# The last layer's FFN as one group of 1024 tokens, with the gated activation kept in DRAM and the down projection summed in PSUM

## The chip, the cores and the metric

One core of a Trainium2 chip runs the whole program: TensorE (PE, with its weight loads as PEld), VectorE (DVE), ScalarE (ACT), GpSimd (POOL), SyncE (SP, which here only issues DMAs), on-chip SBUF, eight accumulation banks of PSUM (128 partitions x 512 fp32 columns each), and DRAM. The metric is the device time of one execution in microseconds (us), as the median of several runs. Beside the times stands one profiled execution with a record of every instruction.

## The reference

A backbone of two layers over 1024 latent tokens and 256 context tokens of width 1024, in fp32. Each layer mixes tokens (three head groups), projects the result (w_out), adds it gated to the stream, and then applies a gated MLP with 22 x 128 = 2816 features whose gate branch passes a centred convolution of width 3 along the tokens. Only latent tokens leave the last layer. In short form:

```python
h = rms_norm(x, g) * (1 + scale) + shift
gate, up = h @ w_gate, h @ w_up                  # (tokens, 2816) each
act = silu(dwconv3(gate, conv_w) + conv_b) * up  # the convolution runs along tokens
x = x + gate_mod * rms_norm(act @ w_down, g2)
```

## The kernel before

**Precision.** Every fp32 operand of a matmul is split into a high and a low part (`split`: a copy that rounds gives the high part, a subtraction the low one), and `mm3` (L246) issues three matmuls: high x high, high x low, low x high. So one product of blocks is three instructions.

**Gate and up.** `ffn` (from L1819) holds the normalised, modulated, transposed input in blocks: the first half of a group's tokens by two halves of the 1024 inputs ("11", "21"), the second half likewise ("22" and a difference "T3"), and from them `ffn_T` makes T1, T2 and T4 (tiles `T`, `ts`). Gate and up of one 128-feature block f are then got with seven products P1 to P7 (`PROD`) of combined weights and combined inputs instead of eight. Each product sums four 128-row blocks, so it takes 12 matmuls, and one f takes 84. The weights of f (`wraw`) are loaded, combined (L1857 to L1860) and split (`fwh`, `wl`, `fsh`, `fsl`) for each f of each group. VectorE combines the products out of PSUM into `fraw` and `fu` (`add`, L1877).

**Groups.** The last layer handles its 1024 tokens in two groups of 512 (tiles 2 to 5 and 6 to 9, 128 tokens each), each half of a group 256 columns and two more for the convolution's neighbours, so n = 258. The second group's input is prepared by `ffn_second` near the end of the first.

**Activation and down.** For each f: centre tap on GpSimd (L1933), the two other taps on VectorE (L1934, L1935), Silu on ScalarE, the multiply on VectorE (L1937), the split into `ahl`. After each pair of f, `down` multiplies the four token tiles with the two row blocks of w_down (`dr`, split into `dh` and `dl`): per tile and half of the output 6 matmuls of 512 columns into one bank, which VectorE then adds to an accumulator in SBUF (`yacc`, L1966 for the first pair, L1968 after that). Products use four banks ("m"), `down` the other four ("b"). `finish` normalises, scales, adds the residual (`res`) and stores.

**Around it.** Ahead of the FFN stands `outproj`: for each token tile 48 matmuls (tile `ow`, `yh`, `yl`), then `post` (L1574 to L1579: squares, an inverse root in small steps, gate, residual) and a store to DRAM (`scr_x`). `ffn_part` reloads the tiles, transposes them on PE (`hTp`) and splits them into the blocks. The instructions of each engine are put in order by a scheduler; buffers come from pools with a count for each name, so a load is issued once its buffer is free. All loads go through SP's queue, in order.

## Time and profile before

| what | value |
|---|---|
| median of 3 runs | 4708.21 us (4696.83 to 4727.73) |
| the profiled execution | 4714.89 us, span 4712.7 us |
| PE busy | 4242.9 us, 90% of the span |
| VectorE, GpSimd, ScalarE busy | 3227.4, 2328.2, 1849.2 us |
| last layer's FFN, first to last product | 3828.5 to 4691.8 us of the span |
| mean granted clock of PE | 0.887 |

The span is what the profiler saw between the first and the last instruction; the execution's own time lies 2.2 us above it. Busy shares are averages over stages that differ much, so the rows below are mostly cut to one stage. The granted clock is a share of full speed: 1.00 is the upper of two levels (2.4 GHz), 0.50 the lower (1.2 GHz), and a mean in between says that a stretch had both.

### The profile page before, as it was taken

Reading aid. Unit: us, or ns where it says so; the run is one execution under the profiler, and the core shown is the slowest. Engines: PE = TensorE matmul, PEld = TensorE weight load, DVE = VectorE, ACT = ScalarE, POOL = GpSimd, SP = SyncE. Lnnn points to the kernel's source line nnn. Section 1 sums busy time; section 2 is a strip of 40 time slices with the busy share of each in tenths; the row PEclk is TensorE's granted clock in tenths of the full one; section 3 lists DMA queues with packets and bytes.
Section 4 is the critical chain, followed back from the end, with each engine's and each line's share of the span. In section 5 each row is a group of like instructions: output and inputs, shape, how many; then the busy total and the mean of one; then the engine's idle time right before and its main releaser. Section 6 shows DMA issues by size and latency. Waiting matters only on the chain. (4 is left out here: it accounts for less than half of the span.)

```text
span 4712.7 us, 72125 instructions
## 1 busy us (share of the span) xinstructions
PE 4242.9 (90%) x26303; PEld 3318.7 (70%) x26303; DVE 3227.4 (68%) x6313; ACT 1849.2 (39%) x3692; POOL 2328.2 (49%) x2295
## 2 busy tenths in 40 slices
PE   8997988989999899979998997889899889997997
PEld 5885654755567799879986875567555678886886
DVE  4346586666655877887776257766777578888887
ACT  3334454543323333333333344555443233333332
POOL 3336225243443666566654243543444366657664
PEclk9996687885999999989998995879879989998998
DMA  6453223152123322232226453223411323223232
GB/s 206 131 141 99 59 75 97 49 142 60 31 78 116 103 81 81 86 112 86 81 85 165 124 134 83 65 54 77 121 56 29 112 101 90 81 85 107 87 90 85
DMA packets 501921, 441.26 MB, mean 94 GB/s; under 512 B 121652, under 2 KB 434108, under 8 KB 501566
## 3 DMA queue, kind: packets, MB, share of 16 engines
q1 hardware_dynamic: 448350, 381.45, 27.8%
q0 software_dynamic: 21056, 51.26, 4.1%
q10 hardware_dynamic: 32160, 3.94, 0.5%
q8 instruction: 208, 3.41, 0.3%
q14 instruction: 147, 1.20, 0.1%
HBM read 353.02 MB, written 83.51 MB: 93 GB/s over the span
## 5 line engine op out<-in xcount | busy, mean ns | idle before, releaser
L244 DVE TENSOR_TENSOR wl<-wraw,fwh 128x1024 fp32r<-128x1024 f32 x176 | 320.3, 1820 | 160.0 <-ACT fwh L238 159.5
L238 ACT ACTIVATE fwh<-wraw 128x1024 fp32r<-128x1024 f32 x264 | 272.4, 1054 | 297.1 <-DVE wraw L1860 156.7
L248 PE MATMUL m<-h,fwh 128*128 128x322 f32 (+1 forms) x1056 | 321.2, 304 | 15.4 <-ACT fu L1906 8.6
L248 PE MATMUL dn<-dh,ahl 128*128 128x512 f32 x792 | 315.4, 402 | 14.6 <-ACT ahl L238 10.0
L249 PE MATMUL dn<-dl,ahl 128*128 128x512 f32 x792 | 319.0, 403 | 8.8 <-POOL dl L244 8.8
L244 POOL TENSOR_TENSOR gp<-gx,gp 128x512 fp32r<-128x512 f32 x160 | 207.7, 1303 | 238.9 <-DVE gp L240 153.1
L250 PE MATMUL m<-h,wl 128*128 128x322 f32 (+1 forms) x1056 | 318.8, 302 | 4.3 <-DVE wl L244 4.3
L249 PE MATMUL m<-h,fwh 128*128 128x322 f32 (+1 forms) x1056 | 321.3, 304 | 0.0
L244 POOL TENSOR_TENSOR dl<-dr,dh 128x1024 fp32r<-128x1024 f32 x88 | 218.8, 2487 | 202.1 <-ACT dh L238 199.7
L1355 ACT ACTIVATE ds<-ds,dnm 128x512 f32<-128x512 f32 (+1 forms) x400 | 232.5, 581 | 185.2 <-DVE dnm L1377 105.6
L250 PE MATMUL dn<-dh,ahl 128*128 128x512 f32 x792 | 304.4, 399 | 0.0
L248 PE MATMUL m<-T,fwh 128*128 128x322 f32 (+1 forms) x704 | 220.4, 313 | 89.2 <-DVE fraw L1877 77.5
L244 POOL TENSOR_TENSOR wl<-wraw,fwh 128x1024 fp32r<-128x1024 f32 x88 | 229.3, 2606 | 122.8 <-ACT fwh L238 118.9
L1419 ACT ACTIVATE p<-ds 128x512 f32<-128x512 f32 (+1 forms) x336 | 186.8, 585 | 254.3 <-PE ds L1418 205.7
L1968 DVE TENSOR_TENSOR yacc<-dn,yacc 128x512 f32<-128x512 f32 x360 | 231.3, 681 | 28.0 <-PE dn L250 28.0
L244 POOL TENSOR_TENSOR ahl<-cv,ahl 128x642 fp32r<-128x642 f32 (+1 forms) x88 | 131.8, 1498 | 226.2 <-ACT ahl L238 203.4
L1936 ACT ACTIVATE cv<-cv 128x642 f32<-128x642 f32 (+1 forms) x88 | 60.6, 688 | 466.4 <-DVE cv L1935 466.4
L1377 DVE TENSOR_REDUCE dnm<-ds 128x1 f32<-128x512 f32 x256 | 173.7, 687 | 90.3 <-PE ds L1375 87.5
L244 DVE TENSOR_TENSOR wl<-wr,wh 128x512 fp32r<-128x512 f32 (+1 forms) x76 | 66.9, 882 | 242.2 <-ACT wh L238 151.0
L250 PE MATMUL m<-T,wl 128*128 128x322 f32 (+1 forms) x704 | 215.9, 307 | 8.5 <-DVE wl L244 8.5
L244 POOL TENSOR_TENSOR wl<-wr,wh 128x512 fp32r<-128x512 f32 (+1 forms) x76 | 100.3, 1319 | 244.6 <-ACT wh L238 175.2
L249 PE MATMUL m<-T,fwh 128*128 128x322 f32 (+1 forms) x704 | 217.3, 309 | 2.3 <-DVE T L244 2.3
(499 smaller groups left out, 13558.7 us busy)
## 6 DMA issues: line engine op xcount, KB each, us to landing
wraw<-in_ff_w_gate_dram SPq DMA_DIRECT2D x88, 512.0 KB
wraw<-in_ff_w_up_dram SPq DMA_DIRECT2D x88, 512.0 KB
dr<-in_ff_w_down_dram SPq DMA_DIRECT2D x88, 512.0 KB
aw<-in_ada_w_dram SPq DMA_DIRECT2D x160, 256.0 KB
wr<-in_w_in_dram SPq DMA_DIRECT2D x88, 256.0 KB
x<-scr_x SPq DMA_DIRECT2D x28, 512.0 KB
scr_df<-st SPq DMA_DIRECT2D x80, 128.0 KB
scr_gq<-st SPq DMA_DIRECT2D x18, 512.0 KB
```

Source lines behind the costliest of these rows:

```text
L238: nc.scalar.activation(hi, src, AF.Copy)
L244: e.tensor_tensor(out=lo, in0=src, in1=hi, op=ALU.subtract)
L248: mm(out, lh, rh, start=first, stop=False)
L249: mm(out, lh, rl, start=False, stop=False)
L250: mm(out, ll, rh, start=False, stop=last)
L1355: act.activation(s, s, AF.Exp, bias=nm[:, c, m, i:i + 1], accum_out=L[:, c, m, i:i + 1])
L1377: vv.tensor_reduce(out=nm[:, 1 + c, m, i:i + 1], in_=s, axis=AX.X, op=ALU.max, negate=True)
L1419: act.activation(p[:, m, :w], s[:, :w], AF.Exp)
L1936: act.activation(t[:, m], t[:, m], AF.Silu)
L1968: vv.tensor_tensor(out=ys[i][:, hs], in0=ps, in1=ys[i][:, hs], op=ALU.add)
```

## The change

Layer 0's code is kept; all that follows is for the last layer (l = 1).

- `FFN[1]` has one group of n = 512: blocks "11" and "21" hold tiles 2 to 5, "22" and "T3" tiles 6 to 9. Neighbour columns between groups, `edge` and `ffn_second` are not used there.
- The body of `steps` becomes `gate_up`, word for word but for three things: banks are taken from both sets in turn (`self.mb`), the split of the second weight pair has its low part on GpSimd, and q lies in `cv`.
- `ffn_last` runs gate and up for all 22 f, and `tail(f)` after each; it stores the gated activation, 128 features x 1024 tokens, to DRAM (`scr_act`). Then the down projection: two passes of four token tiles, in each over all 22 f with the sum held in the eight banks.
- The output projection's weights lie in `wo`; some of its pools and those of the attention before it get fewer buffers or other places (`ahl` 2 for 3, `y` in `fraw`); the last tile takes its two halves in the other order.

```diff
-        ((258, (((2, 3), ((0, 2, 0, 256),)), ((4, 5), ((1, 0, 0, 256),))),
-          ((0, 0), (0, 1), (1, 257)), (1, 256), 6),
-         (258, (((6, 7), ((0, 2, 0, 256),)), ((8, 9), ((1, 0, 0, 256),))),
-          ((0, 0), (1, 256), (1, 257)), (0, 1), None)),
+        ((512, (((2, 3), ((0, 0, 0, 256),)), ((4, 5), ((0, 256, 0, 256),)), ((6, 7), ((1, 0, 0, 256),)), ((8, 9), ((1, 256, 0, 256),))),
+          (), None, None),),
...
+    def gate_up(self, f, order, blk, res):
...
+            ps = P[p] = self.bk(next(self.mb))[:, :n]
...
+    def ffn_last(self, l, src, A, SH, blk, todo, rows):
...
+        def tail(f, raw, q):
+            w3 = [self.pt[:, 28 + NF * t + f:29 + NF * t + f] for t in range(3)]
+            t = ft([128, W], "cv", 4)
+            act.activation(t, raw, AF.Identity, scale=w3[1], bias=self.pt[:, 94 + f:95 + f])
+            vv.scalar_tensor_tensor(out=t[:, 1:W], in0=raw[:, 0:W - 1], scalar=w3[0], in1=t[:, 1:W], op0=ALU.mult, op1=ALU.add)
+            vv.scalar_tensor_tensor(out=t[:, 0:W - 1], in0=raw[:, 1:W], scalar=w3[2], in1=t[:, 0:W - 1], op0=ALU.mult, op1=ALU.add)
+            act.activation(t, t, AF.Silu)
+            gp.tensor_tensor(out=t, in0=q, in1=t, op=ALU.mult)
+            gp.dma_start(out=scr[f], in_=t)
+
+        res = [[], []]
+        st = [self.gate_up(f, self.FIRST, blk, res[f]) for f in range(2)]
+        next(st[0])
+        for t0, t1, p in todo:
+            rows(t0, t1)
+            K.together(p)
+        next(st[1])
+        yield
+        self.ffn_T(blk)
+        next(st[0])
+        for f in range(NF):
+            if f > 1:
+                res.append([])
+                st.append(self.gate_up(f, self.LAST if f == NF - 1 else self.ORDER, blk, res[f]))
+            K.together(st[f])
+            tail(f, *res[f])
+        yield
+
+        def operands(f, t0):
+            r, x = ft([128, D], "dr", 3), ft([128, 512], "ar", 3)
+            self.load(r, a["ff_w_down"][l, f * 128:f * 128 + 128, :])
+            self.load(x, scr[f][:, t0:t0 + 512])
+            g, d = ft([128, 2, 512], "ag", 3, F32R), ft([128, 2, D], "dd", 3, F32R)
+            self.split(d[:, 0], d[:, 1], r, "a", "v")
+            self.split(g[:, 0], g[:, 1], x, "a", "p")
+            return g, d
...
+        for t0 in (0, 4):
+            xs = []
+            for t in range(t0, t0 + 4):
+                xs.append(self.al("fB", [128, D], 8, n="res"))
+                self.load(xs[-1], self.xsrc(src, NCTX + t))
+            acc = [[self.bk(b) for b in ("m", "b")] for _ in range(4)]
...
+            for f in range(NF - 2):
+                g, d = operands(f, 128 * t0)
+                for i in range(4):
+                    products(i, f, g, d)
+                if late:
+                    end(*late.pop(0))
+            ops = [(f, *operands(f, 128 * t0)) for f in (NF - 2, NF - 1)]
+            for i in range(4):
+                for o in ops:
+                    products(i, *o)
+                y = acc[i]
+                if t0 == 0:
+                    s = self.al("hA0", [128, 2, 512], 8, n="ys")
+                    act.activation(s[:, 0], y[0], AF.Copy)
+                    vv.tensor_copy(s[:, 1], y[1])
+                    late.append((t0 + i, (s[:, 0], s[:, 1]), xs[i]))
+                else:
+                    end(t0 + i, y, xs[i])
```

`products` issues `mm3` for the two halves of the output of one tile; `end` is `finish` for one tile, in halves, out of PSUM or out of the copy `ys`.

What the scheduler makes of it is shown at three places. In each row stand line, operation, out<-in and shape.

**PE, start of the FFN.** Before, the last matmul of the output projection (`ow`, `yl`) and the first ones of P1 of f = 0 (`h` is the block "11"):

```order
L249 MATMUL b_36370<-ow_35297,yh_36258 128x512
L250 MATMUL b_36370<-ow_35297,yl_36259 128x512
L248 MATMUL m_36537<-h_35310,fwh_36514 128x258
L249 MATMUL m_36537<-h_35310,fwh_36514 128x258
L250 MATMUL m_36537<-h_35310,wl_36515 128x258
```

With the change the same place holds 36 products, P1 and P2 of f = 0 and P1 of f = 1, and then the transposes of tiles 8 and 9 (`x_36501`, `x_36504`); the rows begin with the last of the 36:

```order
L251 MATMUL m_36594<-h_35312,wl_36572 128x512
L1731 MATMUL hTp_36507<-ident,x_36501 128x128
L1731 MATMUL hTp_36512<-ident,x_36501 128x128
L1731 MATMUL hTp_36522<-ident,x_36501 128x128
L1731 MATMUL hTp_36527<-ident,x_36501 128x128
L1731 MATMUL hTp_36507<-ident,x_36504 128x128
```

Before, the transposes of a group's last tiles stood ahead of its products or, for the second group, among those of the first; now they stand between the first products of the only group.

**VectorE, one feature in the steady part.** Before, the weight split of `wl`, the combinations of 258 columns, the weight combinations (`wraw`) and the accumulators (`yacc`) follow each other:

```order
L1859 TENSOR_TENSOR wraw_43516<-ws_43524,wraw_43516 128x512
L1860 TENSOR_TENSOR wraw_43516<-wraw_43516 128x512
L1877 TENSOR_TENSOR fraw_43414<-fu_43330,m_43401 128x258
L244 TENSOR_TENSOR wl_43530<-wraw_43516,fwh_43529 128x1024
L1877 TENSOR_TENSOR fraw_43329<-fraw_43329,m_43416 128x258
L1877 TENSOR_TENSOR fraw_43414<-fu_43330,m_43416 128x258
L1968 TENSOR_TENSOR yacc_41134<-dn_43440,yacc_41134 128x512
L1968 TENSOR_TENSOR yacc_41134<-dn_43448,yacc_41134 128x512
L1968 TENSOR_TENSOR yacc_41151<-dn_43456,yacc_41151 128x512
L1968 TENSOR_TENSOR yacc_41151<-dn_43464,yacc_41151 128x512
L1934 SCALAR_TENSOR_TENSOR cv_43431<-fraw_43329,pt_23577,cv_43431 128x514
L1968 TENSOR_TENSOR yacc_41168<-dn_43472,yacc_41168 128x512
```

With the change, a whole feature:

```order
L1866 TENSOR_TENSOR fraw_37000<-fu_37001,m_37016 128x512
L245 TENSOR_TENSOR wl_37114<-wraw_37109,fwh_37113 128x1024
L1866 TENSOR_TENSOR fu_37001<-fu_37001,b_37030 128x512
L1848 TENSOR_TENSOR wraw_37109<-ws_37117,wraw_37109 128x512
L1866 TENSOR_TENSOR fraw_37000<-fu_37001,m_37044 128x512
L1849 TENSOR_TENSOR wraw_37109<-wraw_37109 128x512
L1866 TENSOR_TENSOR fu_37001<-fu_37001,b_37058 128x512
L1866 TENSOR_TENSOR cv_37085<-fu_37001,m_37072 128x512
L1866 TENSOR_TENSOR fraw_37000<-fraw_37000,b_37087 128x512
L1866 TENSOR_TENSOR cv_37085<-fu_37001,b_37087 128x512
L1934 SCALAR_TENSOR_TENSOR cv_37102<-fraw_37000,pt_23577,cv_37102 128x1023
L1935 SCALAR_TENSOR_TENSOR cv_37102<-fraw_37000,pt_23577,cv_37102 128x1023
```

The accumulators, one weight split and the multiply are gone from the queue; the combinations are 512 wide and the two taps 1023.

**SP, the end of gate and up.** Before, the loads of weights of gate and up (`wraw`) and of down (`dr`) and of the residuals (`res`) alternate to the end:

```order
L209 DMA dr_43852<-in_ff_w_down_dram 128x1024
L209 DMA wraw_44001<-in_ff_w_up_dram 128x8x128
L209 DMA wraw_44212<-in_ff_w_gate_dram 128x8x128
L209 DMA dr_43858<-in_ff_w_down_dram 128x1024
L209 DMA wraw_44213<-in_ff_w_up_dram 128x8x128
L209 DMA res_44348<-scr_x_102 128x1024
```

With the change, from the last weights of gate and up on:

```order
L210 DMA wraw_39387<-in_ff_w_gate_dram 128x8x128
L210 DMA wraw_39388<-in_ff_w_up_dram 128x8x128
L210 DMA gate_39527<-scr_mod_90 128x1024
L210 DMA res_39531<-scr_x_102 128x1024
L210 DMA res_39533<-scr_x_102 128x1024
L210 DMA res_39535<-scr_x_102 128x1024
L210 DMA res_39537<-scr_x_102 128x1024
L210 DMA res_40307<-scr_x_102 128x1024
L210 DMA res_40309<-scr_x_102 128x1024
L210 DMA res_40311<-scr_x_102 128x1024
L210 DMA dr_39547<-in_ff_w_down_dram 128x1024
L210 DMA ar_39548<-scr_act_36407 128x512
```

The down weights' loads all stand behind gate and seven residuals; the buffers of `dr`, `dd`, `ar` and `ag` come from a pool that opens when that of `T2`, `T14` and `cv` closes.

## Rows read from the trace of the kernel before

**Rows 1.** The page's first part: busy time, share of the span, instructions.

```profile
PE 4242.9 (90%) x26303; PEld 3318.7 (70%) x26303; DVE 3227.4 (68%) x6313; ACT 1849.2 (39%) x3692; POOL 2328.2 (49%) x2295
```

**Rows 2.** Timeline of PE: start us, us, instruction, out<-in, tile, shape.

```profile
3828.49 0.28 PE L248 MATMUL m<-h,fwh 128*128 128x258 f32 x1
...
4382.81 0.29 PE L248 MATMUL m<-T,fwh 128*128 128x258 f32 x1
...
4392.91 0.39 PE L248 MATMUL dn<-dh,ahl 128*128 128x512 f32 x1
4393.14 0.39 PE L249 MATMUL dn<-dl,ahl 128*128 128x512 f32 x1
...
4683.26 0.63 PE L248 MATMUL dn<-dh,ahl 128*128 128x512 f32 x1
4683.69 0.63 PE L249 MATMUL dn<-dl,ahl 128*128 128x512 f32 x1
```

**Rows 3.** Stretches of the last FFN: us, busy (instructions) by engine, clock, DMA, GB/s.

```profile
3828.50:4691.80 863.30, 747.98 (x4785) 679.21 (x4783) 709.97 (x921) 290.69 (x405) 561.52 (x353) 0.94 0.30 91
...
3828.50:3886.00 57.50, 41.71 (x262) 39.13 (x261) 53.63 (x81) 21.63 (x36) 46.04 (x29) 0.76 0.42 138
...
4240.00:4320.00 80.00, 49.01 (x260) 42.33 (x260) 68.31 (x98) 26.74 (x45) 59.43 (x38) 0.81 0.35 113
4320.00:4660.00 340.00, 309.99 (x2043) 283.44 (x2044) 280.80 (x341) 115.14 (x153) 224.16 (x132) 0.97 0.30 90
...
4692.00:4712.70 20.70, 0.00 (x0) 0.00 (x0) 14.60 (x36) 1.15 (x2) 6.92 (x6) 0.61 0.33 127
```

The engines' columns are PE, PEld, DVE, ACT and POOL, in this order.

**Rows 4.** PE's waits, 4320 to 4660 us: releaser, us in total, times, longest.

```profile
PE m L248 <- DVE fraw L1877: 18.2, 8, 2.6
PE m L248 <- DVE fu L1877: 7.3, 8, 1.5
```

**Rows 5.** POOL's groups, 4320 to 4660 us: busy, mean ns, idle before.

```profile
L244 POOL TENSOR_TENSOR wl<-wraw,fwh 128x1024 fp32r<-128x1024 f32 x20 | 51.3, 2566 | 73.1 <-ACT fwh L238 69.6 <-PE dn L250 3.5
L244 POOL TENSOR_TENSOR dl<-dr,dh 128x1024 fp32r<-128x1024 f32 x18 | 44.6, 2476 | 4.5 <-ACT dh L238 4.5
...
L244 POOL TENSOR_TENSOR ahl<-cv,ahl 128x514 fp32r<-128x514 f32 x19 | 25.6, 1348 | 31.7 <-ACT ahl L238 31.7
```

**Rows 6.** DVE's groups, 4320 to 4660 us.

```profile
L244 DVE TENSOR_TENSOR wl<-wraw,fwh 128x1024 fp32r<-128x1024 f32 x39 | 82.1, 2104 | 31.0 <-ACT fwh L238 30.9
L1968 DVE TENSOR_TENSOR yacc<-dn,yacc 128x512 f32<-128x512 f32 x68 | 43.5, 681 | 0.0
...
L1877 DVE TENSOR_TENSOR fraw<-fu,m 128x258 f32<-128x258 f32 x76 | 31.7, 417 | 2.8 <-PE m L250 1.1
L1935 DVE SCALAR_TENSOR_TENSOR cv<-fraw,pt,cv 128x514 f32<-128x514 f32 x18 | 27.3, 1516 | 0.3
```

**Rows 7.** Line 1934, 3880 to 4712 us: shortest, median and longest in ns.

```profile
L1934 DVE SCALAR_TENSOR_TENSOR cv<-fraw,pt,cv x42: 749/1775/3557, 3894.2 to 4676.8; 128x514 f32<-128x514 f32 x42
```

**Rows 8.** Stretches elsewhere: layer 0's FFN, and attention in layer 1.

```profile
1600.00:1900.00 300.00, 300.00 (x1750) 279.11 (x1749) 234.84 (x297) 101.33 (x123) 185.35 (x106) 1.00 0.27 80
3740.00:3760.00 20.00, 19.14 (x90) 15.44 (x89) 11.68 (x55) 6.90 (x19) 5.08 (x4) 1.00 0.57 200
```

**Rows 9.** Timelines of SP, ACT and POOL near the end.

```profile
4669.03 0.33 SPq L209 DMA_DIRECT2D dr<-in_ff_w_down_dram  x1
...
4672.51 1.06 ACT L238 ACTIVATE dh<-dr 128x1024 fp32r<-128x1024 f32 x1 [6.29 <-DMA dr<-in_ff_w_down_dram]
...
4707.11 0.53 POOL L2000 DMA_DIRECT2D out_dram<-yacc  x1 [2.61 <-DVE yacc L1999]
```

**Rows 10.** Timelines of DVE and SP: the last tile's norm and its store.

```profile
3835.79 0.68 DVE L1574 TENSOR_TENSOR oss<-oss 128x1 f32<-128x1 f32 x1
...
3849.01 1.40 DVE L1579 SCALAR_TENSOR_TENSOR po<-b,ors,gate 128x512 f32<-128x512 f32 x2
...
3853.34 0.33 SPq L209 DMA_DIRECT2D scr_x<-xr  x1
```

More of the change, by code (lines that the diff above doesn't have):

```diff
@@ L1638, in outproj @@
                 self.load(gate, self.scr_mod[l][1 if t < NCTX else 0, 2048:3072].partition_broadcast(128))
-            o = []
-            for h in range(2):
-                ps = self.bk("op" if t in OPX else "b")
+            o = [None, None]
+            for h in (1, 0) if last and t == NT - 1 else (0, 1):
+                o[h] = ps = self.bk("op" if t in OPX else "b")
                 for k in range(KD):
@@ L1658, in outproj @@
                 self.together(ready[0][2])
-            if t < NT - 1:
+            if last or t < NT - 1:
                 end()
                 done = t + 1
+        if last:
+            return blk, todo, rows
         for t0, t1, p in todo:
@@ L1729, in ffn_part @@
                     nc.scalar.activation(h, ps[:, t0:t0 + w], AF.Identity, scale=A[:, s, k:k + 1], bias=SH[:, s, k:k + 1])
[L1730 removed]
+                    if self.l == 0 and tiles[-1] == 4 and half and r > 1:
                         nc.gpsimd.tensor_copy(self.edge[:, k:k + 1], h[:, w - 1:w])
@@ L1817, with blocks, add @@
     LAST = ("P6", "P5", "P4", "P1", "P2", "P3", "P7")
+    def gate_up(self, f, order, blk, res):
+        nc, a, l = self.nc, self.a, self.l
+        vv, act, gp = nc.vector, nc.scalar, nc.gpsimd
+        ft = lambda sh, tag, bufs, dt=F32: self.al(tag, sh, bufs, dt)
+        n = self.FFN[l][0][0]
+        W = 2 * n
+        eng = lambda e: vv if e == "v" else gp
+        wg, wu = (ft([128, KD, 128], "wraw", 3) for _ in range(2))
+        for w, nme in ((wg, "ff_w_gate"), (wu, "ff_w_up")):
+            self.load(w, a[nme][l, :, f * 128:f * 128 + 128].rearrange("(k p) c -> p k c", p=128))
+        pair = lambda: (ft([128, KD, 128], "fwh", 3, F32R), ft([128, KD, 128], "wl", 3, F32R))
+        wt = {}
+        def blocks(names, p):
+            for i, b in enumerate(names):
+                wt[b] = [x[:, 4 * i:4 * i + 4] for x in p]
+        x = pair()
+        self.split(*x, wg, "a", EX)
+        blocks(("11", "12"), x)
+        s1 = ft([128, 4, 128], "ws", 1)
+        eng(E1).tensor_tensor(out=s1, in0=wu[:, 0:4], in1=wu[:, 4:8], op=ALU.add)
+        eng(E3).tensor_tensor(out=wu[:, 0:4], in0=wg[:, 0:4], in1=wu[:, 0:4], op=ALU.subtract)
+        eng(E2).tensor_tensor(out=wg[:, 0:4], in0=s1, in1=wg[:, 0:4], op=ALU.subtract)
+        eng(E4).tensor_tensor(out=wg[:, 4:8], in0=wg[:, 4:8], in1=wg[:, 0:4], op=ALU.subtract)
+        y = pair()
+        self.split(*y, wg, "a", "p" if l == DEPTH - 1 else EY)
+        blocks(("S2", "S4"), y)
+        z = pair()
+        self.split(*z, wu, "a", EZ)
+        blocks(("S3", "22"), z)
+        s = ft([128, 4, 128], "fsh", 1, F32R), ft([128, 4, 128], "fsl", 1, F32R)
+        self.split(*s, s1, "a", ES)
+        blocks(("S1",), s)
+        raw, q = ft([128, W], "fraw", 2), None
+        u = ft([128, n], "fu", UB)
+        r1, r2 = raw[:, :n], raw[:, n:]
+        P = {}
+        def add(o, x, y, op=ALU.add):
+            vv.tensor_tensor(out=o, in0=x, in1=y, op=op)
+        for p in order:
+            wb, hb = self.PROD[p]
+            (wh, wl), h = wt[wb], blk[hb]
+            ps = P[p] = self.bk(next(self.mb))[:, :n]
+            for k in range(4):
+                self.mm3(ps, wh[:, k], wl[:, k], h[k][:, 0], h[k][:, 1], k == 0, k == 3)
+            if order is self.LAST:
+                if p == "P6":
+                    act.activation(u, ps, AF.Copy)
+                elif p == "P5":
+                    q = ft([128, W], *(("cv", 4) if l == DEPTH - 1 else ("fraw", 2)))
+                    q2 = q.rearrange("p (a c) -> p a c", a=2)
+                    add(r2, u, ps)
+                    add(q[:, n:], u, ps)
+                elif p == "P4":
+                    add(q[:, :n], u, ps, ALU.subtract)
+                elif p == "P1":
+                    act.activation(r1, ps, AF.Copy)
+                    add(r2, r2, ps)
+                    add(q2, q2, ps.unsqueeze(1).broadcast_to([128, 2, n]))
+                elif p == "P2":
+                    add(r1, r1, ps)
+                elif p == "P3":
+                    add(r2, r2, ps)
+                elif p == "P7":
+                    add(q2, q2, ps.unsqueeze(1).broadcast_to([128, 2, n]))
+            elif p == "P1":
+                act.activation(u, ps, AF.Copy)
+            elif p == "P2":
+                add(r1, u, ps)
+                if order is self.FIRST:
+                    yield
+            elif p == "P6":
+                add(u, u, ps)
+                if "P3" in P:
+                    add(r2, u, P["P3"])
+                    add(u, u, P["P7"])
+            elif p == "P3" and "P6" in P:
+                add(r2, u, ps)
+            elif p == "P7":
+                if "P6" in P:
+                    add(u, u, ps)
+                else:
+                    yield
+            elif p == "P4":
+                q = ft([128, W], *(("cv", 4) if l == DEPTH - 1 else ("fraw", 2)))
+                add(q[:, :n], u, ps, ALU.subtract)
+            elif p == "P5":
+                add(r2, r2, ps)
+                add(q[:, n:], u, ps)
+        res += [raw, q]
@@ L1929, in steps @@
+                res = []
+                yield from self.gate_up(f, order, blk, res)
+                raw, q = res
                 yield
@@ L2109, in run @@
             steps = self.op_weights(l)
-            for _ in range(13):
+            for _ in range(12 if last else 13):
                 next(steps)
@@ L2116, in run @@
             A2 = self.modT(l, 1)
+            self.mb = itertools.cycle(("m", "b") if last else ("m",))
+            if last:
+                self.last_layer(l, src, mid, A2, df_p, op_e, ff_w)
+                for es in (ff_r, p_b, ff_c, in_a, base):
+                    es.close()
+                break
             hT, end = self.outproj(l, src, mid, A2)
```

164 lines of the change are left out of this document (66 added, 98 removed).

## Prediction

> **What bounds the kernel now.** I read four views, from the widest to the narrowest. The page's first part says that the tensor engine (PE) is busy for 90% of the span [rows 1]; that is an average, so the stages of the part that changes were cut out of the span next. The last layer's FFN runs from its first product at 3828.49 us [rows 2] to 4691.8 us, 863.3 us, and the span ends 20.9 us later: 884.2 us in all [rows 3]. In these 863.3 us PE is busy for 748.0, so it idles for 115.3 us, and not evenly: 15.8 in the first 57.5 us, 31.0 in the 80 us where the two groups meet, 30.0 of 340 in a steady stretch of the second group [rows 3]. A stage that idles is also granted a lower clock: 0.76 and 0.81 in these two places, 0.97 in the steady stretch.
>
> What would PE need if nothing held it up? 84 products of 258 columns took 10.10 us, from 4382.81 to 4392.91, or 0.1203 us each; two of 512 columns stand 0.23 us apart (0.231 over a longer row of them) [rows 2]. The stage has 2 groups x 22 features x 84 products (3696 x 0.1203 = 444.6 us) and 1056 of the down projection (1056 x 0.231 = 243.9 us): 688.5 us. So 863.3 - 688.5 = 175 us are lost to idling, the slower clock and looser spacing.
>
> What PE waits for in the steady stretch is named by its waits: 25.5 us of them end with a VectorE combination of products (L1877) [rows 4]. VectorE is busy for 280.8 of 340 us there [rows 3], 83%, with 19 features done (the count of the activation's split, [rows 5]): 17.9 us per feature, where PE needs 84 x 0.1203 + 24 x 0.231 = 15.6. Its queue serves three masters in turn: weight preparation, product combination, and the down accumulators (L1968). So PE sets the time, but VectorE's order and load set how well it is fed.
>
> **The change part by part.** *Gate and up products.* 1848 products of 512 columns take the place of 3696 of 258: 1848 x 0.231 = 426.9 against 444.6 us, so by themselves 18 us. [...]
>
> *What feeds them.* Per feature VectorE gives up four accumulations (68 in 19 features, beside 8 first copies: 4 x 0.68 = 2.7 us) and one of its two weight splits (2.1 us, now on GpSimd), and takes on seven combinations of 512 columns instead of 258 (7 x (0.68 - 0.42) = 1.8 us, the 0.68 from L1968, the same operation at that width) and two convolution taps twice as wide (1.78 + 1.52 = 3.3 us) [rows 6, 7]. From 280.8/19 = 14.8 that makes 14.8 - 2.7 - 2.1 + 1.8 + 3.3 = 15.1 us. GpSimd goes from 224.2/19 = 11.8 to 13.6: it loses the splits of the down weights (2.48) and of the activation (1.35), gets one more weight split and the gating multiply at 2.57 each [rows 5] and the issue of a store, 0.5 [rows 9]. PE now needs 84 x 0.231 = 19.4 us per feature. So VectorE falls from 83% to 78% of PE's time and GpSimd stands at 70%. The nearest stretch in which to see whether PE runs without a gap at such shares is 300 us of layer 0: VectorE 78%, GpSimd 62%, PE busy for all 300 us, clock 1.00 [rows 8]. Also the down products no longer stand between the feature's products, and eight banks instead of four hold these. I take 430 us, between 427 (no gap) and 440 (the clock of 0.97 that the steady stretch was granted). The 22 stores (11.5 MB) hide under a DMA share of 0.30 [rows 3]; nothing reads them before the phase ends.
>
> *Down projection.* 1056 products as before, 243.9 us, now in two passes of 22 features x 24. One feature takes 24 x 0.231 = 5.54 us, and needs its 512 KB weight row block and 256 KB of stored activation: 0.786 MB, 142 GB/s. From 3740 to 3760 us 200 GB/s moved at a DMA share of 0.57 [rows 8]. ScalarE needs 1.06 us for one high part and half of it for the other, VectorE 2.1 and GpSimd 1.35 for the low parts [rows 5, 6, 9]: all well under 5.54. I take 246, between 244 and 250.
>
> *Where the phases meet.* This is the new wait. On SP's queue the first load of a weight row block stands behind the gate and seven residual loads; its buffers lie where the convolution's stood, so it waits for the last feature's multiply. Every later operand load is queued behind it, and PE has nothing else. The chain behind the last product: the centre tap 1.06 (ScalarE's time for that width), two taps 3.3, Silu 1.06, GpSimd's multiply 2.57 [rows 5, 7, 9], 3.48 from the issue of a load to the start of the split that it feeds, and 1.06 for the split [rows 9]; the last feature's other products cover 12 x 0.231 = 2.8. That is 1.06 + 3.3 + 1.06 + 2.57 + 3.48 + 1.06 - 2.8 = 9.7 us, and the eight loads ahead (4.2 MB) can only lengthen it. I take 13; from 9 to 22, the 22 being those 4.2 MB at 200 GB/s (21 us) with load, split and cover. Before, no such place existed, but the groups' meeting and its 31.0 us go.
>
> *Start.* Before, the first group needed tiles 2 to 5 only, and the last tiles' work ran under its products. Now tiles 8 and 9 must pass the norm, go to memory, come back and be transposed before P3 of feature 0. On PE 36 products (8.3 us) cover that, in some positions 48. The chain as it stood before: from 3835.79 to 3850.4 us for the norm, the store issued at 3853.34, so 24.8 us after the first FFN product took over from the last output product, much of it other work between its steps [rows 2, 10]; a reload hop adds 3.5, and the T blocks are twice as wide. I take a loss of 20 us, from 10 (the chain without that other work) to 31 (24.8 + 3.5 + 11 for transposes, splits and one T block, less 8.3).
>
> *Output projection.* Two of its pools shrink (two residual buffers for three) and it gets tile 9's transposes. A tile's 48 products (11.1 us) cover a load hop of 3.5 us; uncovered it would be 8 x 3.5 = 28 us, which I exclude, as the load is issued in the middle of the tile before. I take 2, from 0 to 4.
>
> *End.* Behind the last product stands one tile's norm, where before 20.9 us followed: squares, a chain of small VectorE steps, two halves scaled, added, stored. The last store was issued 5.6 us before the span's end [rows 9]. I take 14, from 11 to 21.
>
> **Sum:** 2 + 20 + 430 + 13 + 246 + 14 = 725 us against 884.2, a gain of 159. The profiled execution took 4714.89 us, so 4556; the median of the runs lies 6.7 us below it, so 4549, and I say 4550. The low ends give 701 (4525), the high ends 768 (4592).
>
> **The rivals.** *A, VectorE held up by GpSimd bounds the first phase.* For: the same tap took from 749 to 3557 ns for the same 514 columns [rows 7]; both taps now are twice as wide and meet more GpSimd work. The Trainium skill ("SBUF — State Buffer", section "Who interferes with whom") says that a VectorE operation with two SBUF inputs contends with a GpSimd one that reads SBUF, and that one of the two blocks fully; the spread of that row agrees. If both taps took the worst time at twice its width, 2 x 7.1 instead of 6.6 us, a feature would cost VectorE 15.1 + 7.6 = 22.7 us, 3.3 over PE, x 22 = 73 us: 4623. Against: that is the worst of 42, and layer 0's stretch runs full with the same kinds of work. 0.13.
>
> *B, the down phase is fed one feature at a time.* Load hop 3.48, high part 1.06, low part 2.1 in a row: 6.6 us per feature instead of 5.54, x 44 = +47: 4597. Against: three buffers of each operand. 0.10.
>
> *C, the change does not do what it says:* PE's waits come from the order in which VectorE takes its work, not from the work between the products. Then the idle share of 30 in 340 stays in the first phase, 427/0.91 = 469, +39: 4589. Against: layer 0's stretch. 0.10.
>
> *D, slower than before.* The down phase has no other work for PE, so if loads come late the clock falls too: at the lower level products stand 0.43 us apart (4683.26 and 4683.69, [rows 2]), 24 x 0.43 = 10.3 us per feature, x 44 - 244 = +210: 4760. It decides at 159/44 = 3.6 us over 5.54, that is when 0.786 MB takes over 9.1 us (86 GB/s). For: every operand load stands in one queue behind the boundary's. Against: 200 GB/s in [rows 8]. 0.03.
>
> **How the numbers follow.** My forecast has 0.64, with 4525 to 4592 of its own. A to C hold 0.33, so the range reaches past A, to 4632; at the low end it goes 10 us further than my own, since the runs of before themselves lie 31 us apart: 4515. One per cent (47 us) is about what a measurement of this kernel can tell from no change. Only D lies on the slow side; 0.05 for A with several high ends at once, so 0.92 faster, 0.05 same, 0.03 slower.
>
> **What would show it.** In the first phase a feature every 19.4 us on PE at a clock of 1.00 (A: 22 to 23, with taps over 5 us; C: 21). In the down phase 22 features in 122 us, PE waiting for no load (B: 146; D: clock near 0.5). One gap of 9 to 22 us ahead of the first down product that ends with a load or its split, and about 20 us of idle in the first 60 us. I would be wrong above all if VectorE's two-input operations met GpSimd's at every feature, or if the start's chain through memory were longer than 40 us.

## The result, and the profile after

The changed kernel takes 4560.66 us (median of 4 runs, 4550.52 to 4579.93); the kernel before took 4702.66 us (4 runs, 4696.83 to 4727.73). The ratio is 0.969, with a 95% interval of 0.964 to 0.974. The forecast was 4550.

The profiled execution took 4560.47 us with a span of 4558.6. The page's first part, answering [rows 1]:

```profile
PE 4169.8 (91%) x24447; PEld 3182.7 (70%) x24447; DVE 2917.1 (64%) x5849; ACT 1797.8 (39%) x3586; POOL 2180.7 (48%) x2151
```

The share of PE hardly moves; the stages tell more. These are stretches of the changed FFN (columns as in [rows 3]): its first 57.5 us, 340 us of gate and up, the place where the phases meet, the down phase, and what follows the last product:

```profile
3822.60:3880.10 57.50, 41.71 (x138) 29.41 (x137) 48.83 (x64) 15.76 (x27) 42.09 (x30) 0.78 0.14 46
3880.10:4220.10 340.00, 339.55 (x1469) 276.10 (x1468) 230.30 (x221) 120.45 (x128) 233.57 (x127) 1.00 0.26 82
...
4280.00:4294.30 14.30, 0.09 (x1) 0.00 (x0) 4.29 (x4) 2.74 (x3) 2.92 (x2) 0.68 0.96 360
4294.30:4537.20 242.90, 242.28 (x1056) 199.47 (x1056) 85.92 (x142) 80.68 (x120) 98.01 (x64) 0.99 0.45 148
4537.20:4558.60 21.40, 0.06 (x1) 0.00 (x0) 10.47 (x34) 0.85 (x4) 10.95 (x13) 0.59 0.26 98
```

PE is busy for 339.55 of 340 us where it was busy for 310 of 340, at a clock of 1.00 instead of 0.97, and a product of 512 columns takes 340/1469 = 0.2314 us. In place of the 25.5 us of [rows 4], PE's waits in gate and up from 3880.1 us on are two:

```profile
PE b L249 <- ACT T L239: 0.2, 1, 0.2
PE m L249 <- ACT fwh L239: 0.2, 1, 0.2
```

From the first product (3822.6) to the end the FFN takes 736.0 us, against 884.2. This is the length that the experiments below compare, because it leaves out what varies ahead of it: at the last `od<-p,vh` product of the attention before it (3638.6 and 3627.0 us) the two profiled executions are already 11.6 us apart.

VectorE's and GpSimd's groups in the same 340 us, answering [rows 5, 6]:

```profile
L245 DVE TENSOR_TENSOR wl<-wraw,fwh 128x1024 fp32r<-128x1024 f32 x18 | 43.4, 2409 | 23.0 <-ACT fwh L239 23.0
L1934 DVE SCALAR_TENSOR_TENSOR cv<-fraw,pt,cv 128x1023 f32<-128x1023 f32 x18 | 40.3, 2238 | 16.3 <-ACT cv L1933 16.3
L1935 DVE SCALAR_TENSOR_TENSOR cv<-fraw,pt,cv 128x1023 f32<-128x1023 f32 x18 | 39.3, 2184 | 0.6
```

```profile
L245 POOL TENSOR_TENSOR wl<-wraw,fwh 128x1024 fp32r<-128x1024 f32 x36 | 86.3, 2401 | 66.9 <-ACT fwh L239 66.9
L1937 POOL TENSOR_TENSOR cv<-cv,cv 128x1024 f32<-128x1024 f32 x18 | 46.5, 2585 | 28.0 <-ACT cv L1936 27.8
```

The two taps take 2.24 and 2.18 us, 4.4 together, where the sum had 6.6. Twice the width cost them little, because a good part of the times of [rows 6, 7] was waiting (see below).

The gap between the phases, in the chain that ended last (start, us, what):

```profile
4277.14 0.24 PE m L251
4277.41 0.70 DVE fraw L1866
4278.18 1.25 ACT cv L1933
4279.45 1.28 DVE cv L1934
4280.74 1.13 DVE cv L1866
4281.87 1.21 DVE cv L1935
4283.16 1.06 ACT cv L1936
4284.30 2.34 POOL cv L1937
4286.66 0.33 SPq L210
4287.05 6.56 DMA ar<-scr_act
4293.63 0.64 ACT ag L239
4294.31 0.79 PE m L249
```

It is the chain that the prediction wrote down, with one combination of products (the second L1866) between the taps. The taps took 2.5 us instead of 3.3, the load 6.6 instead of 3.5, at a DMA share of 0.96. Ahead of it stood the seven residual loads (3.7 MB, issued from 4276.0 us on), behind it the next operands' loads; which of them slowed it isn't shown.

### The profile page after: what moved, and what is told of

It is laid out like the page before. It is cut to its first block, busy times and chain, and to the rows that moved or that the text cites. A ratio compares the mean times of both kernels' runs of the same rounds, so it can differ in the third digit from the quotient of the medians.

```text
span 4558.6 us, 67583 instructions
## 1 busy us (share of the span) xinstructions
PE 4169.8 (91%) x24447; PEld 3182.7 (70%) x24447; DVE 2917.1 (64%) x5849; ACT 1797.8 (39%) x3586; POOL 2180.7 (48%) x2151
## 4 chain that ended last, share of the span: by engine, by line
PE 73%; DVE 13%; DMA 5%; ACT 3%; issue 3%; POOL 2%; SPq 1%; ACTq 0%; DVEq 0%; POOLq 0%
PE m L249 6%; PE m L250 6%; PE m L251 6%; PE b L249 3%; PE b L250 3%; PE od L1432 3%; PE b L251 3%; PE gs L1499 2%; PE gram L955 2%; PE dn L249 2%; PE dn L250 2%; PE dn L251 2%; PE ds L1419 2%; PE gs L1498 2%; PE fm L249 2%
## 5 line engine op out<-in xcount | busy, mean ns | idle before, releaser
L245 DVE TENSOR_TENSOR wl<-wraw,fwh 128x1024 fp32r<-128x1024 f32 x110 | 196.8, 1790 | 114.0 <-ACT fwh L239 111.8
L249 PE MATMUL m<-h,fwh 128*128 128x322 f32 (+1 forms) x660 | 219.8, 333 | 11.0 <-ACT fu L1895 6.8
L250 PE MATMUL m<-h,fwh 128*128 128x322 f32 (+1 forms) x660 | 220.1, 334 | 0.0
L1425 DVE SCALAR_TENSOR_TENSOR p<-p,ls 128x512 f32<-128x512 f32 (+1 forms) x168 | 144.8, 863 | 95.3 <-ACT p L1420 93.3
L1432 PE MATMUL od<-p,vh 128*64 128x512 f32 (+1 forms) x336 | 191.0, 707 | 13.4 <-DVE p L1425 9.2
L1376 PE MATMUL ds<-ks,qs 96*128 96x512 f32 x256 | 155.5, 625 | 44.5 <-ACT ds L1356 37.5
L250 PE MATMUL dn<-dl,ahl 128*128 128x512 f32 x440 | 177.5, 403 | 4.4 <-POOL dl L245 4.4
L249 PE MATMUL dn<-dh,ahl 128*128 128x512 f32 x440 | 175.3, 402 | 5.2 <-ACT ahl L239 3.8
L245 POOL TENSOR_TENSOR dl<-dr,dh 128x1024 fp32r<-128x1024 f32 x44 | 109.5, 2489 | 143.2 <-ACT dh L239 143.2
L249 PE MATMUL m<-T,fwh 128*128 128x322 f32 (+1 forms) x436 | 147.1, 338 | 32.7 <-DVE fraw L1866 23.7
L251 PE MATMUL dn<-dh,ahl 128*128 128x512 f32 x440 | 171.4, 399 | 0.0
L1419 PE MATMUL ds<-qs,ks 104*128 104x512 f32 (+1 forms) x336 | 152.7, 496 | 8.8 <-ACT p L1420 5.9
```

Source lines behind the costliest of these rows:

```text
L245: e.tensor_tensor(out=lo, in0=src, in1=hi, op=ALU.subtract)
L249: mm(out, lh, rh, start=first, stop=False)
L250: mm(out, lh, rl, start=False, stop=False)
L251: mm(out, ll, rh, start=False, stop=last)
L1376: mm(s, us["q"][m][0:96, i * 128:i * 128 + 128], K2[m][0:96, 256 + 512 * c:768 + 512 * c], start=True, stop=True)
L1419: mm(s[:, :w], hs["K"][m][0:104, j * 128:j * 128 + 128], us["q"][m][0:104, :w], start=True, stop=True)
```

## The experiments

Twelve kernels were run, eleven of them once, the last one six times. "FFN" is the time from its first product to the end of the span, 884.2 us before and 736.0 changed. How well one execution shows a stage can be read from stages that an edit leaves alone: from the first to the last product of gate and up the change, `res_later` and `tail` take 457.5, 457.7 and 457.6 us, and behind the last product the six kernels with the same end take 21.3 to 21.5 us.

**What held PE before.** Two edits of the kernel before take work away beside the weight preparation; in the first the sums go:

```diff
-                        else:
+                        elif not last:
                             vv.tensor_tensor(out=ys[i][:, hs], in0=ps, in1=ys[i][:, hs], op=ALU.add)
```

> The kernel before, in whose last layer the sums of the down products into the accumulators are left out (all but the first pair of features; the output is then not the reference's). VectorE loses 2.7 of 14.8 us per feature, PE keeps all its products. Theory 1, VectorE's load: PE waited because VectorE's queue was too full, so the steady feature falls from 17.9 to between 15.7 and 16.3 us, and the FFN from 863 by 65 to 90 us. Theory 2, order and banks: PE waited because down products stand among the others and each kind has only four banks; then the steady feature stays at 17.5 to 18 and the FFN within 15 us of 863.

In the second all down products after the first pair go:

```diff
-                    for h in range(2):
+                    for h in range(0 if last and f0 else 2):
```

> The kernel before, in whose last layer all down products after the first pair of features are left out with their sums: the two kinds of products are apart, but groups stay two and products 258 columns wide. PE needs 10.1 us per feature, VectorE 14.8 - 2.7 = 12.1. Theory 3, width: to separate the phases would not have been enough, VectorE bounds the narrow products, 12.0 to 13.0 us per feature and PE idle for 16 to 22% of a steady stretch. Rival: the products alone run at PE's rate, 10.1 to 10.7 us per feature.

Steady stretches of the two, the first without the sums, the second without down products:

```profile
4310.00:4650.00 340.00, 306.03 (x1996) 280.51 (x1995) 246.97 (x319) 116.00 (x156) 216.09 (x131) 0.96 0.30 87
```

```profile
4230.00:4570.00 340.00, 254.49 (x1728) 246.37 (x1728) 267.94 (x339) 124.80 (x167) 239.15 (x140) 0.86 0.31 95
```

Without the sums VectorE's busy time falls from 280.8 to 247.0 us and nothing is gained: the first taps (L1934) of every second feature start 36.2 us apart, before 36.3, so a feature takes 18.1 us in both (the 17.9 of the prediction counts 19 features into 340 us), and the FFN takes 880.1. So theory 1 falls: 2.7 us off VectorE's queue per feature are worth nothing. Without the down products, in the second kernel, PE idles for 25% of the stretch, with 20 features in it, 17.0 us each where PE needs 10.1 and VectorE by its own sum 12.1. So neither PE's work nor VectorE's own, nor the order of two kinds of products alone, made a feature take 17 to 18 us. Separating the phases at the old width would not have gained either, by an estimate: 44 features at 17.0 us and 243.9 us of down products are 992 us, and at 14.7 us, the shortest stretch of this run (below), 891, against 884.2. In this second kernel PE's waits over the same stretch name ScalarE, which is busy for 125 us of it:

```profile
PE m L248 <- ACT fwh L238: 72.8, 18, 6.8
PE m L248 <- DVE fraw L1877: 11.7, 5, 4.6
```

The next two edits go at the preparation of the weights and at GpSimd. In the first, a feature with an odd number takes over its neighbour's prepared weights (`prepare` is the old block of loads, combinations and splits):

```diff
+                if last and f % 2 and f > 1:
+                    wt.update(self.wprev)
+                else:
+                    prepare()
+                self.wprev = wt
```

> The kernel before, in whose last layer each odd feature from 3 on uses the prepared weights of the feature before it (loads, combinations and splits of its own are left out; the output is then not the reference's); groups, widths, down products and their sums stay. After the first four runs theory 1 is out (without the sums the steady feature took 18.4 us) and the narrow products alone took 18.2 us per feature on a PE that was busy for 75%. Theory 3, preparation: what holds PE before is the preparation of each feature's weights by GpSimd, VectorE and ScalarE for only 512 tokens. With half of it the steady feature falls from 17.9 to 15.7 to 16.6 us, and the FFN from 863 by 50 to 95 us. Rival, the convolution and the combinations hold it: 17.2 to 18.2 us per feature, and less than 30 us.

In the second, preparation is whole, and GpSimd no longer makes the low parts for the down products:

```diff
-                self.split(hi, lo, r, "a", ED)
+                if last:
+                    act.activation(hi, r, AF.Copy)
+                    lo = hi
+                else:
+                    self.split(hi, lo, r, "a", ED)
```

The same is done for the activation's split.

> The kernel before, in whose last layer GpSimd does not make the low parts of the down projection's two operands (the high parts stand in for them, so PE has the same products and the output is not the reference's); the preparation of the gate and up weights stays whole. GpSimd loses 2.48 + 1.35 of 11.8 us per feature, about as much as half the preparation took from it. Theory 3 in its narrow form, the preparation as a chain of steps with few buffers holds PE: then this changes little, 17.2 to 18.2 us per feature and less than 30 us of the FFN's 863. Theory 4, the load that GpSimd and VectorE share: less work on GpSimd serves as well as half the preparation did (15.8 us per feature, 98 us less): 15.8 to 16.6 us and 60 to 100 us less.

Steady stretch and one VectorE group of each, half preparation first:

```profile
4270.00:4560.00 290.00, 290.00 (x1977) 268.93 (x1976) 197.78 (x298) 81.65 (x111) 142.33 (x89) 1.00 0.22 66
...
L244 DVE TENSOR_TENSOR wl<-wraw,fwh 128x1024 fp32r<-128x1024 f32 x18 | 23.8, 1325 | 5.5 <-ACT fwh L238 5.5
```

```profile
4280.00:4560.00 280.00, 280.00 (x1917) 260.48 (x1916) 228.38 (x325) 113.19 (x144) 142.19 (x88) 1.00 0.34 102
...
L244 DVE TENSOR_TENSOR wl<-wraw,fwh 128x1024 fp32r<-128x1024 f32 x35 | 45.4, 1298 | 32.8 <-ACT fwh L238 32.8
```

Both run PE without a gap, 15.8 us per feature, and both take the FFN down by 97 to 98 us (to 786.3 and 787.1), the first a little more than was expected of it. So the preparation as a chain of steps does not hold PE by itself: taking a similar amount from GpSimd elsewhere serves as well. That leaves theory 4, the load that GpSimd and VectorE share. These two runs take work from GpSimd, and alone they could not tell that sharing from a queue of GpSimd that is too long; the instructions can. The split of `wl` on VectorE takes 2104 ns before [rows 6] and 1298 ns when GpSimd has less to do, while the sum L1968, which reads one operand from PSUM and one from SBUF, took 681 ns before and 682 ns here.

Two of these splits in the kernel before, and two of GpSimd's:

```profile
4336.14 1.21 DVE L244 TENSOR_TENSOR wl<-wraw,fwh 128x1024 fp32r<-128x1024 f32 x1
...
4338.48 2.22 DVE L244 TENSOR_TENSOR wl<-wraw,fwh 128x1024 fp32r<-128x1024 f32 x1
```

```profile
4321.32 2.47 POOL L244 TENSOR_TENSOR wl<-wraw,fwh 128x1024 fp32r<-128x1024 f32 x1 [2.73 <-ACT fwh L238]
...
4336.21 3.40 POOL L244 TENSOR_TENSOR wl<-wraw,fwh 128x1024 fp32r<-128x1024 f32 x1 [3.33 <-ACT fwh L238]
```

GpSimd's second split began 0.07 us after VectorE's and took 0.9 us longer than its first; VectorE's second began while that one had 1.1 us to go and took 1.0 us longer. The whole stretch from 4320 to 4660 us holds 132 VectorE operations that read two tiles in SBUF. The 58 that began while GpSimd was idle stay within 0.02 us of the shortest of their kind; the 64 that began with more than 0.25 us of a GpSimd operation on two tiles to go are longer than that by what was to go, less 0.12 to 0.19 us. GpSimd's operations that began inside one of VectorE's are longer in the same way, less 0.07 to 0.15 us in 49 of 50. So the later one waits for the earlier. That is the rule of the Trainium skill ("SBUF — State Buffer", section "Who interferes with whom"): such a VectorE operation and a GpSimd one that reads SBUF contend, and the second to start is blocked until the first is done; the trace agrees, but for that overlap of 0.07 to 0.19 us.

Busy time thus holds waiting for the other engine, on both sides, and an estimate of what the two need goes by shortest times. For VectorE (shortest, median, longest):

```profile
L244 DVE TENSOR_TENSOR wl<-wraw,fwh x39: 1210/2121/3415, 4320.3 to 4655.7; 128x1024 fp32r<-128x1024 f32 x39
...
L1935 DVE SCALAR_TENSOR_TENSOR cv<-fraw,pt,cv x42: 741/1635/4548, 3896.0 to 4677.6; 128x514 f32<-128x514 f32 x42
...
L1859 DVE TENSOR_TENSOR wraw<-ws,wraw x40: 676/685/1818, 3904.8 to 4651.9; 128x512 f32<-128x512 f32 x40
```

Per feature these are two splits of 1.21, taps of 0.75 [rows 7] and 0.74, two weight combinations of 0.68 (L1859, L1860) and the multiply, as wide, of 0.68: 5.95 us. GpSimd's busy 11.8 us are 10.7 by shortest times (two splits of 2.4, four operations of 1.28 to 1.29 and the centre tap of 0.77). Together that is 16.6 of the 18.1 us that a feature took, and in 45.7 of the 340 us neither ran. So what GpSimd and VectorE must do in turn took most of the time; what held the other 1.5 us is not shown. The sums, out of PSUM, are outside this account, and leaving them out changed nothing.

The run without down products has a test of it. Nothing holds GpSimd to one weight block of w_down per feature there, so it splits 20 of them during the 12 features of the first stretch and has none left for the five of the second, while VectorE does nearly the same work in both:

```profile
4266.50:4484.10 217.60, 152.42 (x1007) 147.34 (x1007) 176.43 (x226) 81.99 (x109) 164.72 (x92) 0.84 0.34 105
...
4498.80:4573.60 74.80, 59.88 (x423) 58.21 (x422) 54.43 (x71) 25.64 (x35) 44.20 (x32) 0.89 0.24 71
```

That is 18.1 us per feature with these splits and 15.0 without, on a PE that is not full in either; by shortest times the two engines need 18.2 and 14.2 us. The first group of that run repeats it (18.0 and 14.7 us). For the changed kernel the same estimate gives 11.6 us of GpSimd, and for VectorE one split of 1.21, two taps of 1.28 and two combinations of 0.68: 16.8 us, under PE's 19.4.

**Load and banks in the changed kernel.**

```diff
+                if l == DEPTH - 1 and order is self.ORDER:
...
+                    for _ in range(4):
+                        add(self.yd, ps, self.yd)
```

With the second weight split's low part back on VectorE as well:

> The changed kernel with VectorE's old load put back in the steady part of gate and up: the second weight split's low part again on VectorE (about 2.4 us), and four sums of 128x512 out of PSUM per feature into a scratch tile (2.7 us). VectorE goes from about 12.9 to 18.0 us of the 19.4 that PE needs, 93%. Theory 1, load: PE begins to wait, 20.0 to 21.5 us per feature, 12 to 40 us more in the stage. Theory 2, order and banks: no wait as long as VectorE stays under PE, 19.4 to 19.7 us per feature, 0 to 6 us more.

Products in four banks (`itertools.cycle(("m",))`):

> The changed kernel with gate and up products in four banks instead of eight; the down projection keeps eight. Theory 2: PE waits for combinations to free banks, 20.0 to 21.5 us per feature, 12 to 45 us more in the stage. Theory 1: four banks hold four products of 2.8 us each, which is longer than VectorE is ever late, 19.4 to 19.7 us per feature, 0 to 6 us more.

Gate and up from 57.5 us after the first product on, with the load put back, and the first two stretches with four banks:

```profile
3910.40:4250.40 340.00, 335.82 (x1447) 273.44 (x1447) 275.81 (x299) 119.64 (x127) 200.52 (x109) 0.99 0.25 81
```

```profile
3829.90:3887.40 57.50, 34.74 (x110) 21.29 (x108) 48.98 (x65) 16.87 (x28) 42.97 (x30) 0.81 0.15 46
3887.40:4227.40 340.00, 339.84 (x1466) 277.21 (x1467) 232.34 (x214) 117.39 (x126) 226.74 (x125) 0.99 0.26 81
```

Neither matters in the steady part. With VectorE at 81% (GpSimd loses 2.4 us per feature by the moved split) PE loses one wait of 4.2 us, and the FFN takes 740.2, 4 more. That wait ends 79 us after the first product, and `keep` and `hi_scalar` below have the same one without any load put back, so it isn't shown to come from the load. Four banks cost 7 us (742.8), all in the start: 110 products and transposes in the first 57.5 us instead of 138.

**The start.** `keep` hands tiles 8 and 9 on in SBUF (`kept` is the buffer in which the output projection left the tile); `hi_scalar` moves eight copies from VectorE:

```diff
-            self.load(x, self.xsrc(src, t)[:r])
+            if kept is None:
+                self.load(x, self.xsrc(src, t)[:r])
...
-                        self.split(o[:, 0, c0:c0 + w], o[:, 1, c0:c0 + w], h, "v", "p")
+                        self.split(o[:, 0, c0:c0 + w], o[:, 1, c0:c0 + w], h, "a" if self.l == DEPTH - 1 and tiles[-1] == NT - 1 else "v", "p")
```

> The changed kernel with tiles 8 and 9 taken for the transposes from the buffers that the output projection leaves them in, instead of being read back from DRAM; they are still stored. In the chain of the start the store and the reload took 2.6 and 3.3 us. If the chain through memory sets the start, the 25.6 us that the first 57.5 us of the FFN lose fall by 5 to 7. If VectorE's T blocks alone set it (it was busy from 3842 to 3883 us with hardly a gap), they begin earlier by the same amount but another wait takes its place: less than 3 us.

> The changed kernel with the high parts of the blocks of tiles 8 and 9 made by ScalarE instead of VectorE (eight small operations, 6.5 us in VectorE's row of the start). Keeping tiles 8 and 9 on the chip did not shorten the start (the FFN without its tail took 461.7 instead of 457.3 us up to the last gate and up product), so the trip through memory is not what sets it. If VectorE's queue in the start sets it, the stretch up to the last gate and up product falls by 3 to 7 us; if GpSimd's part of the same steps does, by less than 2 us.

Up to the last gate and up product, `keep` and then `hi_scalar`:

```profile
3827.90:4289.60 461.70, 441.32 (x1865) 353.21 (x1863) 320.00 (x320) 154.91 (x175) 304.05 (x174) 0.97 0.23 74
```

```profile
3843.80:4306.50 462.70, 442.75 (x1865) 353.15 (x1863) 313.65 (x312) 157.85 (x183) 303.55 (x174) 0.97 0.24 75
```

Both end 4 to 5 us behind the 457.3 of the change. Their first 70 us are not slower, though; here the change and `keep` (`hi_scalar` has 188 products and transposes in them):

```profile
3822.60:3892.60 70.00, 53.76 (x183) 38.05 (x182) 58.73 (x77) 20.60 (x32) 50.84 (x34) 0.80 0.15 46
```

```profile
3827.90:3897.90 70.00, 53.78 (x193) 37.49 (x192) 58.62 (x77) 20.74 (x33) 47.93 (x33) 0.88 0.12 38
```

By then `keep` is 10 products ahead, 2.3 us, and `hi_scalar` 5. Then both meet a wait that the change does not have, which ends 78 and 79 us after the first product (the row is the same in both):

```profile
PE m L249 <- ACT fwh L239: 4.2, 1, 4.2
```

So the trip through memory cost the start some 2 us, as the second reading of `keep` expected, and VectorE's copies about 1, and a later wait for weights takes back more than either gives. Neither sets the start. What does stays open: with the copies moved, PE's waits there go to GpSimd's low parts of T and hT (4.9 us), which fits the shared load but is not shown.

**Where the phases meet.** `res_later` moves the residual loads in the program; `both` also places the operands:

```diff
+                if f == 4:
+                    for t in range(t0, t0 + 4):
+                        xs.append(self.al("fB", [128, D], 8, n="res"))
+                        self.load(xs[-1], self.xsrc(src, NCTX + t))
...
-            r, x = ft([128, D], "dr", 3), ft([128, 512], "ar", 3)
+            r, x = ft([128, D], "wraw", 3), ft([128, 512], "T14", 4)
...
-            g, d = ft([128, 2, 512], "ag", 3, F32R), ft([128, 2, D], "dd", 3, F32R)
+            g, d = ft([128, 2, 512], "T2", 4, F32R), (ft([128, D], "fwh", 3, F32R), ft([128, D], "wl", 3, F32R))
```

> The changed kernel with the residual loads of the down phase moved behind the operands of four features. Two causes are mixed in the 14.2 us between the phases: the tail of the last feature, whose buffers the first operands take, and 4 MB of loads ahead of them. If the tail alone sets the issue of the first load, that still comes some 7 us after the last product, but lands in 3.5 us instead of 6.6: the gap falls to 10.5 to 12.0 us. If the loads ahead set it, the gap falls below 8 us.

> As the run before, and the operands of the down phase also take buffers that are free before the last products (weights in those of the gate and up weights, activations in those of T2 and T14). Then neither the tail nor the loads stand ahead: the gap between the phases falls from 14.2 to between 0 and 3 us, and the down phase keeps its 243 us. If instead the first operands are late for another reason (SP's order, DRAM), over 6 us stay. If the T14 buffers, which are now loaded ahead, hold up the weight loads behind them on SP, the down phase takes 246 to 260 us.

SP's queue of `res_later`, then the meeting of the phases in `both`:

```profile
4282.08 4.40 SPq L210 DMA_DIRECT2D res<-scr_x  x7
4292.70 0.33 SPq L210 DMA_DIRECT2D dr<-in_ff_w_down_dram  x1
```

```profile
4303.20:4315.00 11.80, 11.80 (x52) 9.49 (x51) 7.52 (x7) 5.16 (x6) 4.14 (x3) 1.00 1.00 391
4315.00:4552.40 237.40, 235.06 (x1007) 188.48 (x1005) 81.91 (x145) 75.05 (x113) 90.75 (x60) 1.00 0.42 142
```

`res_later` decided nothing: the scheduler issued the seven loads where they had been, since they were ready while the first operand was not, and PE's wait is 12.8 us instead of 14.2. In `both` it is gone, PE is busy for all of the 11.8 us. The down phase gives 6 us back (249.2 us: one wait of 2.3, and products 0.233 us apart instead of 0.230), so the FFN takes 728.0, 8 less.

**The end.**

```diff
-                gp.tensor_tensor(out=o, in0=o, in1=x[:, c], op=ALU.add)
-                gp.dma_start(out=self.out[0, t * 128:t * 128 + 128, c], in_=o)
+                (vv if t > 3 else gp).tensor_tensor(out=o, in0=o, in1=x[:, c], op=ALU.add)
+                (nc.sync if t > 3 else gp).dma_start(out=self.out[0, t * 128:t * 128 + 128, c], in_=o)
```

> The changed kernel with the residual's sum of the last four token tiles on VectorE instead of GpSimd, and their stores on SP's queue. Now 21.4 us follow the last product. If GpSimd's sums (2.5 us per tile) and its stores set the end, it falls to 14 to 18 us. If VectorE's small steps and scalings set it (some 5 us per tile, four tiles, from the first tile's last product on), the sums come on top of these, and it stays at 19 to 23 us.

Behind the last product, with the edit:

```profile
4520.50:4534.70 14.20, 0.00 (x0) 0.00 (x0) 9.99 (x34) 0.77 (x3) 0.00 (x0) 0.64 0.31 118
```

14.2 us instead of 21.4. GpSimd's sums and stores set the end (which of the two is not separated), although VectorE now does the sums: next to GpSimd's, single steps of 0.16 us on 128x1 had taken up to 1.2 us. The FFN takes 728.5.

**Together.**

> The changed kernel with three of the edits tried above together: residual loads behind the first operands, operands in buffers that are free before the last products, the last four tiles' residual sums on VectorE and their stores on SP's queue. Each removed its wait alone: the first two brought the FFN with its tail from 736.0 to 728.0 us, the third the tail from 21.4 to 14.2 us. If the waits add up, the FFN with its tail takes 719 to 723 us and the median falls by 13 to 17 us below the changed kernel's 4561. If the tail now waits for residuals that are loaded later, or the down phase loses on SP's queue, half of it is lost: 725 to 732 us.

The FFN takes 720.8 us, 15.2 less than with the change alone; the 8.0 of `both` and the 7.5 of `tail` are 15.5, so the waits add up. The median is 4540.01 us (6 runs, 4527.48 to 4560.59), a ratio to before of 0.966 (0.963 to 0.970). The interval overlaps that of the change, so against the change only the FFN's 15.2 us are shown, not a difference of the medians.

## Why the prediction was right, step by step

- **Sum.** 725 us were forecast, 723 of them for the FFN, and 736.0 measured. The medians lie 142.0 us apart where 159 were forecast; 4560.66 is 11 above the forecast and inside its own range. The misses cancel in part: start, meeting and end took 18 us more than their terms, the other three 7 less.
- **Gate and up, 430.** 1848 x 0.2314 is 427.6. The size was right. The reason given was half right: PE does run full, but not because VectorE's load falls from 83% to 78%. It fell to 68%, and `b_no_acc` shows that its load was not the limit. The sum of 15.1 us per feature (230.3/18 = 12.8 measured) had the taps at 6.6 instead of 4.4 and left out that the multiply, 0.68, goes to GpSimd; nothing came of it, since PE set the time. What the change took away is half of the weight preparation, and with it work that GpSimd and VectorE can't do at once. Layer 0's stretch [rows 8], which decided the term, was a good witness all the same, probably because it has the same kinds of work on both engines.
- **Start, 20.** The stage up to the last gate and up product took 457.3 us, so 457.3 - 427.6 = 29.7 us were lost, next to the upper bound of 31. This is the largest miss, 10 us, in the term whose mechanism was wrong. The prediction made the chain through memory the long part and allowed 11 us for transposes, splits and one T block. The chain was short:

```profile
3835.87 3.27 DMA x<-scr_x
3839.16 0.77 DVE x L1717
```

The tile was back 16.6 us after the first product, where the upper bound had 28. The splits and T blocks were long: on VectorE they ran from 3841.6 to 3883.9 us. By their shortest times they need 20 of the 38 us that they took; the rest they waited for GpSimd, as in these two rows of one line, of which only the first began during a GpSimd operation:

```profile
3856.85 1.75 DVE L1805 TENSOR_TENSOR ts<-ts 128x512 f32<-128x512 f32 x1
...
3875.09 0.69 DVE L1805 TENSOR_TENSOR ts<-ts 128x512 f32<-128x512 f32 x1
```

How much of the 10 us that is, no run shows.

- **Meeting of the phases, 13.** 14.2, by the chain that was written down, with the load longer and the taps shorter than taken.
- **Down, 246.** 242.9.
- **Output projection, 2.** Not settled. From the last `od<-ident,ms` product of the attention to the first FFN product it is 275.8 us against 274.3, and 268 to 276 in the runs of either kernel. From the last `gs<-gq,kg` product, nearer by, it is 122.2 against 116.2, and 119 to 122 in all nine changed kernels against 115 to 116 in all five of before; so some 5 us lost there are won ahead of it, and what the output projection has of that is not separated.
- **End, 14.** 21.4. The step counted one tile's norm; but four tiles finish within 9 us on PE, and VectorE and GpSimd together need 4 to 5 us for each.
- **Rivals.** A named the right mechanism at the wrong place: it took most of the time before, and after the change it is at 16.8 of 19.4 us. Its price, the worst tap doubled, was far too high (2.2 us, not 7.1). B and D: three buffers held, with 148 GB/s and PE's clock at 0.99. C's premise was true in part (the sums between the products were not what PE waited for), its conclusion not.

## What to carry to other kernels

Beside each engine's busy share, add up the shortest times of GpSimd's operations and of VectorE's with two inputs in SBUF (busy times hold the waiting for each other): where the sum comes near the period, as 16.6 of 18.1 us here, these two are the first suspects, whatever the waits name. To take work off GpSimd, or more tokens per prepared weight, helped there; to take work out of PSUM off VectorE did not. Where two phases meet, place the second one's first buffers where the first one's are freed early.

## What the runs showed of the hardware

- A VectorE operation with two inputs in SBUF that began during a GpSimd operation on two tiles was longer by what was left of that one, less 0.12 to 0.19 us (64 of 64 in 340 us); one that met none stayed within 0.02 us of the shortest. GpSimd's were lengthened by VectorE's in the same way.
- So a VectorE split of 128x1024 took 1210 to 3415 ns in one kernel, while sums with one operand in PSUM stayed at 675 to 687 ns. VectorE was busy for 83% and GpSimd for 66%, and PE's waits named a VectorE operation that reads PSUM.
- Between the phases 360 GB/s moved at a DMA share of 0.96, and beside loads for later use 256 KB that PE waited for took 6.6 us; 512 KB had taken 3.5 [rows 9].
